# A decoder block in fp32: GLA's output stored ungated and gated in the merge's fetch; shared operands' sums and low parts on VectorE by name, down weights' sums on GpSimd by name

## The chip, the cores and the metric

The kernel runs on one core of one Trainium2 chip, as one program. The metric is the device time of one execution in microseconds. The kernel before has a median of 1993.65 us over 3 runs (1989.53 to 1995.26).

## The reference

One decoder block on 1024 tokens of width 1024, in fp32: a Mamba-2 branch (SSD) and a gated linear attention branch (GLA) side by side, a gated merge, cross attention to 256 memory tokens, and a SwiGLU feed-forward layer (inner width 2816). Cut to what the change touches:

```python
def gla_mixer(q, k, v, r, a1, w_a2, b_a, norm_g):
    ...
    o = (o_intra + o_inter).reshape(Bsz, S, H, dv)
    o = rmsnorm(o, norm_g).reshape(Bsz, S, GLA_DV)
    return (o * jax.nn.silu(r.astype(jnp.float32))).astype(q.dtype)
...
    merged = jax.nn.sigmoid(g_ssd) * (y_ssd @ w_up_ssd) + jax.nn.sigmoid(g_gla) * (y_gla @ w_up_gla)
    return merged @ w_o
...
        h = h + hybrid_mixer(rmsnorm(h, norm_mix[i]), w_in[i], ssd_conv_w[i], ssd_conv_b[i], ssd_dt_bias[i],
                             ssd_A_log[i], ssd_D[i], ssd_norm[i], gla_w_a2[i], gla_b_a[i], gla_norm[i],
                             w_up_ssd[i], w_up_gla[i], w_o[i])
        h = h + mem_cross_attention(rmsnorm(h, norm_xattn[i]), rmsnorm(mem, norm_mem[i]),
                                    w_xq[i], w_xkv[i], w_xo[i])
        h = h + swiglu(rmsnorm(h, norm_ffn[i]), w_ffn_in[i], w_ffn_out[i])
    return rmsnorm(h, norm_final)
```

## The kernel before, in words

**Layout and precision.** Activations are kept transposed: features lie on the 128 partitions, tokens on the free axis (1024, worked in two halves of 512). A matrix of 1024 rows is eight row blocks. A product in fp32 is made of three matmuls: `split` (L223) writes the high part of an operand on ACT (a rounding copy) and its low part on DVE, or on an engine handed to it (a subtraction). Then come high by high, high by low and low by high.

**Two kinds of projections.** `Unit` (L276) with `Operands` (L231) computes a 256-column piece of a projection by seven block products in place of eight, in Winograd's manner. `Operands` holds the right side, shared by all units of a stage: B11, B21, T1, B22, T2, T3, T4, of which the four T's are sums of blocks. `Operands.build` makes for each name and each row block k one sum (`comb`, for the T's) and one split. `Unit.left` makes the sums of weight blocks in the same way (`sa`, `raw`). `dense` (L1191) is the plain form: for each of 16 output tiles 24 matmuls over eight row blocks into one of four PSUM accumulators (`acc`), then `post`.

**Engines by a meter.** `either(ap, slack)` (L85) picks POOL or DVE when the kernel is built, from a rough clock of each engine (`Meter`). It is used in `Operands.build`, `kv_unit`, `v_steps`, `Unit.left`, `presum` and some epilogues. The order of each engine's instructions is then made by the framework's scheduler, from priorities (`ahead`, and `run`, which steps side generators at a rate beside a main one). All DMAs named here are issued by SP, in order, on one queue.

**Stages in time.** 0 to about 190 us: norms of `mem` and `x`, the keys and values of the memory (`kv_unit`, L550, tiles `raw`, `whi`, `wlo`), x turned and scaled into `hs`, the first `Operands` from `hs`, and v with the small columns (`v_steps`, tiles `vraw`, `vsa`). To 640: projections and the SSD scan. 640 to 822: the GLA scan in eight chunks of 128 tokens, beside units of the gates `gs` and `gg`. 837 to 1185: four dense stages (w_up_ssd, w_up_gla, w_o, w_xq). Then cross attention, a fifth dense stage (w_xo), whose output tiles `o` feed the second `Operands`, and the feed-forward layer from about 1330 to the end.

**The GLA scan** (class `GLA`, L998). A chunk loads q and k (`qk`), the decays (`bd`), r (`sr`, 512 KB, written to `sr_d` earlier) and v. `decay` makes exponentials on ACT; `attend` the scores; `out` the output `o`, its mean square, and `o` scaled by its root (ACT, L1067); `norm` turns `o` on PE, and DVE multiplies it with the gain and with Silu(r), which `gate` (L1018) has made on ACT, into `qk`, stored to `yg_d`. ACT loads a function table when it changes between Silu and Exp.

**The merge.** `fetch` (L1213) loads a row block of `ys_d` or `yg_d` into an `hl` tile of 128 x 2 x 1024 and splits it there. The first dense stage computes on `ys_d` while `fetch(yg_d, ...)` runs as a side generator; its epilogue `post_ys` multiplies with Sigmoid of the gate (`gated`, L1286) and stores `ysg_d`. The second adds its own gated product to that and splits it for w_o. The third adds the residual (`residual`, L1300). Gate tiles are `gates` and the weight ring's `whi` and `wlo` (`gate`, L1270); 512-column tiles come from a pool of six, `ga` (`quad`, L1137).

**The down weights.** `presum` (L1239) loads 11 blocks of `in_w_ffn_out` of 1 MB into `pre`, makes four sums of each (`sa`, `pre`) and stores them to `down_d`, beside the first dense stages; `waiting(early, 5)` starts it five steps into the first.

Of the kernel before, what the change touches and what calls it, by code (L numbers as in the profile page):

```python
# [9 lines left out]
F32 = mybir.dt.float32  # L10
# [68 lines left out]
def block_kernel(ctx: ExitStack, tc: tile.TileContext, t: dict, out: bass.AP):  # L79
# [151 lines left out]
    class Operands:  # L231
# [30 lines left out]
        def build(s, hb, kh, first):  # L262
            blk = hb if callable(hb) else lambda: hb
            for name in s.order:
                new, of, comb = s.PLAN[name]
                o = s.B[name] = [slot(s.last_key if name == "T4" else s.key, (P, kh, HALF), F32R, name=name + x) for x in "hl"]
                for k in range(kh):
                    q = lambda ij: blk()[ij[0] * kh + k][:, half(ij[1] ^ s.swap)]
                    for ij in new:
                        first(ij[0] * kh + k, ij[1] ^ s.swap, q(ij))  # L270
                    if comb:
                        comb[0](either(q(of), 1.0), q(of), q(comb[1]), q(comb[2]))
                    split(q(of), o[0][:, k], o[1][:, k], either(q(of)))
                    yield
# [275 lines left out]
    def kv_unit(c0):  # L550
# [7 lines left out]
        for kk in range(4):  # L558
            with ahead():
                hi, lo = wring()  # L560
                hv = hi[:, :512].rearrange("p (k c) -> p k c", c=256)
                lv = lo[:, :512].rearrange("p (k c) -> p k c", c=256)
                split(raw[:, 2 * kk:2 * kk + 2, :], hv, lv, either(lo))
# [73 lines left out]
    def v_steps():  # L637
        for pr in range(2):
# [13 lines left out]
            for n, name in enumerate(CHAIN):  # L652
                parts = []
                with ahead():
                    e = either(A11, 2.0)
                    if name == "T1":
                        add(e, sa, A21, A22)
                    elif name == "B22":
                        sub(e, sa, sa, A11)
                        sub(either(A11, 2.0), A12, A12, sa)  # L660
                    elif name == "T3":
                        sub(e, A21, A11, A21)
# [335 lines left out]
    class GLA:  # L998
# [5 lines left out]
        def load_qk(s):  # L1004
            s.qk = gl.tile([P, 8, CH], F32, name="qk", tag="qk", bufs=2)
# [3 lines left out]
        def load(s):  # L1009
# [3 lines left out]
            s.sr = gl.tile([P, 8, CH], F32, name="sr", tag="sr", bufs=2)  # L1013
            SP.dma_start(s.sr, sr_d[:, tk].rearrange("(k p) s -> p k s", p=P))
            s.v = gl.tile([P, D], F32, name="v", tag="v", bufs=2)
            SP.dma_start(s.v, v_d[tk, :])

        def gate(s):  # L1018
            ACT.activation(s.sr, s.sr, AF.Silu)
# [49 lines left out]
        def norm(s):  # L1069
            for a in range(2):  # L1070
                p = bank()
                for b in range(4):
# [3 lines left out]
                y, g = (x.rearrange("p (b a) s -> p a b s", a=2)[:, a] for x in (s.qk, s.sr))  # L1076
                DVE.scalar_tensor_tensor(y, p.rearrange("p (b s) -> p b s", s=CH), col("gla_norm", a), g,
                                         ALU.mult, ALU.mult)
            SP.dma_start(yg_d[:, s.tk].rearrange("(k p) s -> p k s", p=P), s.qk)

    def gla_steps():
# [10 lines left out]
        it[0].gate()  # L1092
        yield
        for i, a in enumerate(it):
# [4 lines left out]
            if b and i:  # L1099
                b.load_qk()  # L1100
# [10 lines left out]
            if b:  # L1111
                b.gate()
# [113 lines left out]

    get_ys = fetch(ys_d, i_ys, "ssd_norm")
# [11 lines left out]
    def presum():  # L1239
# [3 lines left out]
        for k in range(KP):  # L1243
# [5 lines left out]
            e = lambda: either(s1_, 1.0)  # L1249
            add(e(), s1_, a(1, 0), a(1, 1))  # L1250
            put(0, s1_)
            yield
            sub(e(), a(1, 1), s1_, a(0, 0))
            put(1, a(1, 1))
            yield
            sub(e(), a(1, 0), a(0, 0), a(1, 0))
            put(2, a(1, 0))
            yield
            sub(e(), a(0, 1), a(0, 1), a(1, 1))
# [26 lines left out]
    def gated(g, p):  # L1286
        ACT.activation(g, g, AF.Sigmoid)
        mul(DVE, g, p, g)
# [11 lines left out]
    def residual(store, stats, gain, put):  # L1300
        def post(o, j, p, q):
            add(DVE, q, p, q)
# [18 lines left out]
    run(dense(0, i_ys, post_ys, lambda o, j: gate(gs_d, o, j)), (fetch(yg_d, i_yg), 0.5), (waiting(early, 5), 1.0))  # L1321
    run(dense(1, i_yg, post_yg, lambda o, j: (gate(gg_d, o, j), quad(ysg_d, o * P, 0, j))), (early, 1.0))
    run(dense(2, i_wo, residual(h1_d, s1, "norm_xattn", put_xq), quad_of(xT_d)), (early, 1.0))


# [356 lines left out]
```

## Time and profile before

| | |
|---|---|
| median of 3 runs | 1993.65 us (1989.53 to 1995.26) |
| the profiled execution | 1992.12 us |
| its span in the trace | 1990.4 us |
| granted TensorE clock, mean | 0.992 |
| PE busy | 1933.6 us |
| DVE, ACT, POOL busy | 1315.8, 867.6, 659.7 us |
| read from and written to HBM | 211.07 and 96.80 MB |

The profiled execution is one run, with its own time; the span runs from its first to its last instruction. In the profile's rows an instruction is named by engine, line, operation, and tiles as out<-in. L73 and L51 are lines of the helper classes through which DVE's, POOL's and PE's instructions pass, so there the tiles tell the place. A row of the timeline has its start, its length, and behind it how long the engine was idle before, with what ended that. "x3" means three instructions shown as one row.

### The profile page before, as it was taken

What the parts mean: (1) busy time and instruction counts of PE and PEld (TensorE: products, weight loads), DVE (VectorE), ACT (ScalarE), POOL (GpSimd) and SP (SyncE); (2) the same over time, 40 slices, a digit from 0 to 9 for tenths busy, and PEclk for the clock granted to TensorE, in tenths of its full rate; (3) what the DMA queues carried; (4) which work ended last, traced back from release to release, by engine and by line L of the source; (5) the groups of instructions that cost most, each with busy time, mean ns of one, the idle gap of its engine ahead of it and who ended that gap; (6) DMA issues with size and microseconds to landing.
All of it is one profiled execution on the core that took longest, in us unless ns stands there. A gap on an engine that the chain in (4) does not pass through costs nothing.

```text
span 1990.4 us, 26272 instructions
## 1 busy us (share of the span) xinstructions
PE 1933.6 (97%) x9772; PEld 1619.8 (81%) x9772; DVE 1315.8 (66%) x1837; ACT 867.6 (44%) x1486; POOL 659.7 (33%) x482
## 2 busy tenths in 40 slices
PE   7899999999999999999999999999999999999998
PEld 6899677787887887888888888877888888878887
DVE  6856579978887665643654227478777777784565
ACT  7434845455552555442223226453333333353243
POOL 3521243445654211122442100255444444420002
PEclk9899999999999999999999999999999999999999
DMA  9332233365563756697774210433224224176463
GB/s 311 137 118 88 95 118 117 106 212 169 179 183 101 217 175 185 214 377 254 253 269 158 70 43 22 153 121 102 80 90 148 80 86 130 60 276 215 155 227 126
DMA packets 242019, 309.59 MB, mean 156 GB/s; under 512 B 16586, under 2 KB 164276, under 8 KB 241892
## 3 DMA queue, kind: packets, MB, share of 16 engines
q1 hardware_dynamic: 241892, 307.92, 46.2%
q8 instruction: 77, 1.26, 0.3%
q14 instruction: 50, 0.41, 0.1%
HBM read 211.07 MB, written 96.80 MB: 155 GB/s over the span
## 4 chain that ended last, share of the span: by engine, by line
PE 71%; DVE 11%; ACT 5%; DMA 5%; issue 4%; POOL 3%; SPq 1%; POOLq 0%; DVEq 0%; ACTq 0%
PE acc L51 63%; PE bank L51 8%; DVE wlo L73 2%; DVE cv L73 2%; DMA raw<-in_w_in_dram 1%; DVE o L73 1%; PE bank L55 1%; ACT whi L224 1%; DMA xt<-in_x_dram 1%; DMA sr<-sr_d 1%; DVE fs L73 1%; DMA fr<-act_d 1%; POOL raw L73 1%; POOL sa L73 1%; DMA yg_d<-qk 1%
## 5 line engine op out<-in xcount | busy, mean ns | idle before, releaser
L51 PE MATMUL acc<-hl,wd 128*128 128x512 f32 x1920 | 438.6, 389 | 0.0
L51 PEld LDWEIGHTS acc<-hl,wd 128*128 128x128 f32 x1920 | 360.1, 188 | 74.3
L73 DVE TENSOR_TENSOR wlo<-raw,whi 128x512 fp32r<-128x512 f32 x264 | 242.3, 922 | 75.5 <-ACT whi L224 75.2
L224 ACT ACTIVATE whi<-raw 128x512 fp32r<-128x512 f32 x272 | 169.6, 627 | 233.9 <-PE acc L51 203.1
L73 DVE TENSOR_TENSOR o<-acc,o 128x512 f32<-128x512 f32 (+1 forms) x256 | 172.8, 676 | 113.7 <-PE acc L51 99.5
L51 PE MATMUL acc<-fs 128*128 128x512 f32 (+1 forms) x792 | 156.0, 356 | 1.7 <-ACT o L1577 1.6
L73 POOL TENSOR_TENSOR raw<-raw,sa 128x512 f32<-128x512 f32 x48 | 65.2, 1358 | 260.9 <-DVE wlo L73 252.3
L51 PEld LDWEIGHTS acc<-fs 128*128 128x128 f32 x792 | 130.7, 189 | 22.8 <-ACT o L1577 2.0
L224 ACT ACTIVATE fs<-fr 128x1024 fp32r<-128x1024 f32 (+1 forms) x84 | 79.9, 984 | 112.8 <-PE acc L51 39.8
L73 DVE TENSOR_TENSOR fs<-fr,fs 128x1024 fp32r<-128x1024 f32 (+1 forms) x84 | 99.7, 1219 | 39.2 <-ACT fs L224 38.9
L224 ACT ACTIVATE whi<-sa 128x512 fp32r<-128x512 f32 x96 | 59.9, 626 | 108.0 <-PE acc L51 106.9
L73 POOL TENSOR_TENSOR sa<-raw 128x512 f32<-128x512 f32 x47 | 77.4, 1647 | 78.4 <-DMA raw<-in_w_in_dram 41.1
L73 DVE TENSOR_TENSOR wlo<-sa,whi 128x512 fp32r<-128x512 f32 x96 | 83.6, 873 | 17.7 <-ACT whi L224 16.2
L224 ACT ACTIVATE wd<-raw 128x1024 fp32r<-128x1024 f32 x40 | 42.4, 1059 | 108.7 <-PE acc L51 105.6
L73 DVE TENSOR_TENSOR wd<-raw,wd 128x1024 fp32r<-128x1024 f32 x40 | 54.9, 1373 | 50.5 <-ACT wd L224 50.2
L73 POOL TENSOR_TENSOR raw<-raw 128x512 f32<-128x512 f32 x48 | 83.4, 1738 | 4.7 <-DVE sa L73 4.7
L51 PE MATMUL acc<-B21h,whi 128*128 128x512 f32 x192 | 76.1, 396 | 3.2 <-ACT o L353 3.2
L51 PE MATMUL acc<-T4h,whi 128*128 128x512 f32 x192 | 76.7, 399 | 1.5 <-DVE o L73 1.5
L51 PE MATMUL acc<-B11h,whi 128*128 128x512 f32 x192 | 75.6, 394 | 2.3 <-ACT whi L224 2.3
L51 PE MATMUL acc<-B22h,wlo 128*128 128x512 f32 x192 | 76.2, 397 | 1.2 <-DVE wlo L73 1.2
L51 PE MATMUL acc<-T1h,whi 128*128 128x512 f32 x192 | 75.6, 394 | 1.7 <-ACT whi L224 1.7
L73 POOL TENSOR_TENSOR o<-o 128x512 f32<-128x512 f32 x29 | 49.2, 1702 | 83.4 <-DVE o L73 72.1
(389 smaller groups left out, 4784.6 us busy)
## 6 DMA issues: line engine op xcount, KB each, us to landing
raw<-in_w_in_dram SPq DMA_DIRECT2D x26, 1024.0 KB, 6.0
raw<-in_w_ffn_in_dram SPq DMA_DIRECT2D x22, 1024.0 KB, 6.1
act_d<-o SPq DMA_DIRECT2D x77, 256.0 KB, 2.1
fr<-act_d SPq DMA_DIRECT2D x35, 512.0 KB, 6.6
pre<-in_w_ffn_out_dram SPq DMA_DIRECT2D x11, 1024.0 KB, 7.4
fr<-down_d SPq DMA_DIRECT2D x20, 512.0 KB, 3.7
down_d<-pre SPq DMA_DIRECT2D x33, 256.0 KB, 4.5
raw<-in_w_xkv_dram SPq DMA_DIRECT2D x8, 1024.0 KB
```

Of the source, the lines that this page charges most:

```text
L51: return s.e.matmul(o, x, y, **kw)
L55: return s.e.transpose(o, x, i)
L73: return f(*a, **kw)
L224: ACT.activation(hi, src, AF.Copy)
```

## The change

Four edits.

1. **Shared operands.** In `Operands.build` the sums and low parts, in `kv_unit` the low parts, and in `v_steps` the sums run on DVE always, where the meter chose before. In the order of instructions this moves from POOL to DVE: 14 sums of `hs`, 8 low parts of the memory's weights, four sums of 128x1056 in `v_steps`, the first operands' low parts that POOL had, and eight operations on `o` at the second `Operands`.
2. **GLA.** The scan no longer loads `sr` nor computes Silu; `norm` evicts the turned `o` by a copy on ACT (16 in all) in place of DVE's multiplication, and `yg_d` holds the ungated output. `qk` has three buffers, loaded one chunk earlier. `fetch_gated` takes the place of `fetch(yg_d, ...)`: for each half row block it loads r, makes Silu (ACT), multiplies with output and gain (DVE) and splits. It makes 16 steps, at a rate of 1.0 for 8 at 0.5, and its r tiles come from the pool `ga`.
3. **The gates.** Sigmoid(x) becomes tanh(x/2) on ACT and (t + 1) * p on DVE, which is twice the gated product; the residual after w_o is scaled by 0.5.
4. **Down weights.** The sums of `presum` run on POOL by name; it starts 12 steps into the first dense stage, and its rate in the next two is 1.1.

The number of matmuls is the same. ACT has 18 table loads for 33.

```diff
--- before.py
+++ after.py
@@ -269,8 +269,8 @@
                     for ij in new:
                         first(ij[0] * kh + k, ij[1] ^ s.swap, q(ij))
                     if comb:
-                        comb[0](either(q(of), 1.0), q(of), q(comb[1]), q(comb[2]))
-                    split(q(of), o[0][:, k], o[1][:, k], either(q(of)))
+                        comb[0](DVE, q(of), q(comb[1]), q(comb[2]))
+                    split(q(of), o[0][:, k], o[1][:, k])
                     yield
 
     class Unit:
@@ -560,7 +560,7 @@
                 hi, lo = wring()
                 hv = hi[:, :512].rearrange("p (k c) -> p k c", c=256)
                 lv = lo[:, :512].rearrange("p (k c) -> p k c", c=256)
-                split(raw[:, 2 * kk:2 * kk + 2, :], hv, lv, either(lo))
+                split(raw[:, 2 * kk:2 * kk + 2, :], hv, lv)
             for i in range(2):
                 o = pa[i][:, :256]
                 for k2 in range(2):
@@ -652,14 +652,13 @@
             for n, name in enumerate(CHAIN):
                 parts = []
                 with ahead():
-                    e = either(A11, 2.0)
                     if name == "T1":
-                        add(e, sa, A21, A22)
+                        add(DVE, sa, A21, A22)
                     elif name == "B22":
-                        sub(e, sa, sa, A11)
-                        sub(either(A11, 2.0), A12, A12, sa)
+                        sub(DVE, sa, sa, A11)
+                        sub(DVE, A12, A12, sa)
                     elif name == "T3":
-                        sub(e, A21, A11, A21)
+                        sub(DVE, A21, A11, A21)
                     a = (A11, A12, sa, A12, sa, A21, A22)[n]
                     for k2 in range(2):
                         hi, lo = wring()
@@ -1002,7 +1001,7 @@
             s.c, s.tk = c, slice(c * CH, (c + 1) * CH)
 
         def load_qk(s):
-            s.qk = gl.tile([P, 8, CH], F32, name="qk", tag="qk", bufs=2)
+            s.qk = gl.tile([P, 8, CH], F32, name="qk", tag="qk", bufs=3)
             for i, d in enumerate((q_d, k_d)):
                 SP.dma_start(s.qk[:, 4 * i:4 * i + 4], d[:, s.tk].rearrange("(k p) s -> p k s", p=P))
 
@@ -1010,13 +1009,8 @@
             tk = s.tk
             s.bd = gl.tile([P, 4, CH], F32, name="bd", tag="bd", bufs=2)
             SP.dma_start(s.bd, bd_d[:, tk].rearrange("(k p) s -> p k s", p=P))
-            s.sr = gl.tile([P, 8, CH], F32, name="sr", tag="sr", bufs=2)
-            SP.dma_start(s.sr, sr_d[:, tk].rearrange("(k p) s -> p k s", p=P))
             s.v = gl.tile([P, D], F32, name="v", tag="v", bufs=2)
             SP.dma_start(s.v, v_d[tk, :])
-
-        def gate(s):
-            ACT.activation(s.sr, s.sr, AF.Silu)
 
         def decay(s):
             e = gl.tile([P, 4, CH], F32, name="e", tag="e", bufs=1)
@@ -1073,9 +1067,8 @@
                     k = 2 * b + a
                     PE.transpose(p[:, b * P:(b + 1) * P], s.o[:, k // 2, (k % 2) * P:(k % 2) * P + P], ident)
 
-                y, g = (x.rearrange("p (b a) s -> p a b s", a=2)[:, a] for x in (s.qk, s.sr))
-                DVE.scalar_tensor_tensor(y, p.rearrange("p (b s) -> p b s", s=CH), col("gla_norm", a), g,
-                                         ALU.mult, ALU.mult)
+                ACT.activation(s.qk.rearrange("p (b a) s -> p a b s", a=2)[:, a], p.rearrange("p (b s) -> p b s", s=CH),
+                               AF.Copy)
             SP.dma_start(yg_d[:, s.tk].rearrange("(k p) s -> p k s", p=P), s.qk)
 
     def gla_steps():
@@ -1089,15 +1082,14 @@
         it[0].start()
         yield
         it[0].attend()
-        it[0].gate()
         yield
         for i, a in enumerate(it):
             b = it[i + 1] if i + 1 < len(it) else None
             c = it[i + 2] if i + 2 < len(it) else None
             a.out()
             yield
-            if b and i:
-                b.load_qk()
+            if c:
+                c.load_qk()
             a.scan()
             yield
             if b:
@@ -1108,8 +1100,6 @@
             yield
             if b:
                 b.attend()
-            if b:
-                b.gate()
             if c:
                 c.load()
             yield
@@ -1224,6 +1214,19 @@
                 sub(DVE, x[:, 1], raw, x[:, 0])
             yield
 
+    def fetch_gated(src, gate_src, dst):
+
+        for k in range(NB):
+            x = hl(dst, k)
+            raw = x[:, 1].bitcast(F32)
+            SP.dma_start(raw, src[k * P:(k + 1) * P, :])
+            for j in range(2):
+                g = quad(gate_src, k * P, 0, j)
+                ACT.activation(g, g, AF.Silu)
+                DVE.scalar_tensor_tensor(g, raw[:, half(j)], col("gla_norm", k % 2), g, ALU.mult, ALU.mult)
+                split(g, x[:, 0, half(j)], x[:, 1, half(j)])
+                yield
+
     get_ys = fetch(ys_d, i_ys, "ssd_norm")
     for n, _ in enumerate(group(gg[3:], B)):
         if n == 0:
@@ -1246,17 +1249,16 @@
             a = lambda i, j: r[:, j, half(i)]
             s1_ = sums["m"].tile([P, HALF], F32, name="sa", tag="sa", bufs=2)
             put = lambda n, ap: SP.dma_start(down_d[(n * KP + k) * P:(n * KP + k + 1) * P, :], ap)
-            e = lambda: either(s1_, 1.0)
-            add(e(), s1_, a(1, 0), a(1, 1))
+            add(POOL, s1_, a(1, 0), a(1, 1))
             put(0, s1_)
             yield
-            sub(e(), a(1, 1), s1_, a(0, 0))
+            sub(POOL, a(1, 1), s1_, a(0, 0))
             put(1, a(1, 1))
             yield
-            sub(e(), a(1, 0), a(0, 0), a(1, 0))
+            sub(POOL, a(1, 0), a(0, 0), a(1, 0))
             put(2, a(1, 0))
             yield
-            sub(e(), a(0, 1), a(0, 1), a(1, 1))
+            sub(POOL, a(0, 1), a(0, 1), a(1, 1))
             put(3, a(0, 1))
             yield
 
@@ -1284,8 +1286,8 @@
         return got_g[n][j]
 
     def gated(g, p):
-        ACT.activation(g, g, AF.Sigmoid)
-        mul(DVE, g, p, g)
+        ACT.activation(g, g, AF.Tanh, scale=0.5)
+        DVE.scalar_tensor_tensor(g, g, 1.0, p, ALU.add, ALU.mult)
 
     def post_ys(o, j, p, g):
         gated(g, p)
@@ -1297,9 +1299,9 @@
         add(either(g), g, g, y)
         into(i_wo, o, j, g)
 
-    def residual(store, stats, gain, put):
+    def residual(store, stats, gain, put, scale=1.0):
         def post(o, j, p, q):
-            add(DVE, q, p, q)
+            DVE.scalar_tensor_tensor(q, p, scale, q, ALU.mult, ALU.add)
             SP.dma_start(store[o * P:(o + 1) * P, half(j)], q)
             put(o, j, q, col(gain, o))
             stats.take(j, q)
@@ -1318,9 +1320,9 @@
             yield
 
     early = presum()
-    run(dense(0, i_ys, post_ys, lambda o, j: gate(gs_d, o, j)), (fetch(yg_d, i_yg), 0.5), (waiting(early, 5), 1.0))
-    run(dense(1, i_yg, post_yg, lambda o, j: (gate(gg_d, o, j), quad(ysg_d, o * P, 0, j))), (early, 1.0))
-    run(dense(2, i_wo, residual(h1_d, s1, "norm_xattn", put_xq), quad_of(xT_d)), (early, 1.0))
+    run(dense(0, i_ys, post_ys, lambda o, j: gate(gs_d, o, j)), (fetch_gated(yg_d, sr_d, i_yg), 1.0), (waiting(early, 12), 1.0))
+    run(dense(1, i_yg, post_yg, lambda o, j: (gate(gg_d, o, j), quad(ysg_d, o * P, 0, j))), (early, 1.1))
+    run(dense(2, i_wo, residual(h1_d, s1, "norm_xattn", put_xq, 0.5), quad_of(xT_d)), (early, 1.1))
 
 
     kv = []
```

## The prediction

> **What bounds the kernel now.** First the share of the span for each engine, and the chain of work that ended last, shared out by engine:
>
> ```profile
> span 1990.4 us, 26272 instructions
> PE 1933.6 (97%) x9772; PEld 1619.8 (81%) x9772; DVE 1315.8 (66%) x1837; ACT 867.6 (44%) x1486; POOL 659.7 (33%) x482
> PE 71%; DVE 11%; ACT 5%; DMA 5%; issue 4%; POOL 3%; SPq 1%; POOLq 0%; DVEq 0%; ACTq 0%
> ```
>
> TensorE is busy 97%. The change touches no matmul, so it can only win or lose inside the 1990.4 − 1933.6 = 56.8 us in which PE is idle, or by the clock that a stall costs. So the second view is what PE waits for (us in all, times, longest), and the third the stages that the change touches (stretch, then length and the busy us of PE, PEld, DVE, ACT and POOL, granted clock, DMA share, GB/s).
>
> ```profile
> PE bank L51 <- DVE wlo L73: 6.4, 1, 6.4
> PE bank L55 <- ACT o L1067: 5.6, 4, 2.4
> ...
> 20.00:50.00 30.00, 24.99 (x189) 22.87 (x188) 22.09 (x33) 23.81 (x48) 18.24 (x14) 0.94 0.93 300
> 20.00:70.00 50.00, 36.01 (x256) 33.48 (x256) 42.09 (x48) 32.79 (x66) 36.71 (x25) 0.86 0.82 275
> 41.07:71.51 30.44, 20.58 (x134) 19.47 (x135) 30.44 (x29) 17.70 (x36) 24.07 (x17) 0.78 0.80 287
> 640.00:825.00 185.00, 179.28 (x864) 150.09 (x863) 114.36 (x221) 96.93 (x198) 43.30 (x36) 0.99 0.56 171
> 837.00:925.00 88.00, 88.00 (x390) 72.84 (x390) 38.38 (x38) 35.91 (x46) 18.21 (x12) 1.00 0.90 332
> 840.00:890.00 50.00, 50.00 (x222) 41.42 (x221) 23.95 (x23) 22.42 (x29) 6.07 (x4) 1.00 1.05 397
> 1330.00:1360.00 30.00, 25.92 (x116) 20.61 (x115) 28.78 (x35) 14.85 (x27) 20.41 (x14) 0.94 0.30 97
> ```
>
> Idle PE time: 50 − 36.01 = 13.99 us early, 185 − 179.28 = 5.7 in the GLA scan, none in the first dense stage (837 to 925), 30 − 25.92 = 4.08 at the FFN's start. Early and at the FFN's start DVE is nearly always busy; in the GLA stage PE waits for ACT; in the first dense stage nothing binds but the DMAs run full (397 GB/s).
>
> **Part 1, shared operands by DVE alone, early.** The longest wait, 6.4 us, is here. DVE, POOL, and the chain's pieces of that stretch:
>
> ```profile
> 23.86 0.49 DVE L73 TENSOR_SCALAR diag<-ident,xr 128x128 f32<-128x128 f32 x2 [1.13 <-POOL xr L73]
> 37.20 2.63 DVE L73 TENSOR_SCALAR diag<-ident,xr 128x128 f32<-128x128 f32 x2
> ...
> 43.05 0.68 DVE L73 TENSOR_TENSOR wlo<-raw,whi 128x512 fp32r<-128x512 f32 x1
> 43.65 0.74 DVE L73 SCALAR_TENSOR_TENSOR hs<-bank,cols,rbc 128x512 f32<-128x512 f32 x1
> ...
> 57.39 3.86 DVE L73 TENSOR_TENSOR T1l<-hs,T1h 128x512 fp32r<-128x512 f32 x3
> 72.33 1.89 DVE L73 TENSOR_TENSOR B22l<-hs,B22h 128x512 fp32r<-128x512 f32 x3
> 36.68 2.87 POOL L73 TENSOR_TENSOR vsa<-vraw 128x1056 f32<-128x1056 f32 x1 [2.89 <-DMA vraw<-in_w_in_dram]
> L73 POOL TENSOR_TENSOR hs<-hs 128x512 f32<-128x512 f32 x14 | 22.7, 1652 | 4.5 <-DVE B11l L73 3.3 <-DVE T1l L73 1.3
> 62.98 6.72 PE bank L51 x34
> 77.00 5.76 PE bank L51 x48
> ```
>
> POOL makes 14 sums of hs, 22.7 us, the bulk of its 24.07 us in 41.07 to 71.51, where DVE never rests. The same DVE operation takes 3.86 us for three while POOL works and 1.89 for three when it doesn't. Alone, a tensor-tensor starts (43.65 − 43.05) 0.60 us before the next. DVE's 29 instructions there are 20 tensor-tensors, 8 scalar-tensor-tensors from PSUM and a small copy: undisturbed 20 × 0.60 + 8 × 0.66 (0.74 less the overlap of 0.08) + 0.2 = 17.5 us. It took 30.44, so 12.9 us of DVE's time go to running beside POOL, 0.92 for each of the 14 sums. Done on DVE a sum costs 0.60: 14 × (0.92 − 0.60) = 4.5 us less on the engine that PE waits for. I take −4.2, since some of POOL's time there (24.07 − 22.7) stays.
> The stall also costs clock: after it, 34 matmuls take 6.72 us (0.198 each) against 5.76 for 48 (0.12), 34 × 0.078 = 2.7 us. A wait shorter by two thirds should save about half: −1.3.
> The kv lows and two sums of 128x1056 go to DVE too. The latter takes 2.87 us on POOL; on DVE I scale 0.60 by 1056/512 to about 1.25 and see the disturbance come back: diag 2.63 beside it against 0.49. I take these moves as even. Sum early: −5.5. Bounds: −12, if nearly all of the 13.99 idle goes (the rest are first loads), and +3, if DVE's extra work comes ahead of what PE needs next, as the first kv low after the stall stands ahead of T1's lows in the new order.
> A rule bears on this. The Trainium skill, "SBUF — State Buffer", section "Who interferes with whom", says that a DVE instruction with two SBUF inputs and a GpSimd instruction that reads SBUF exclude one another, the loser waiting for the whole instruction. By it each sum could cost DVE nearly all of its time on POOL; the 0.92 that the trace gives lies below that. It makes the gain larger (first rival).
>
> **Part 2, the GLA scan.** Groups of ACT and DVE in 640 to 825 (busy, mean ns; then idle before them and its releaser):
>
> ```profile
> L1019 ACT ACT_TABLE_LOAD x8 | 10.3, 1283 | 25.7 <-DMA sr<-sr_d 25.6
> L1019 ACT ACTIVATE sr<-sr 128x1024 f32<-128x1024 f32 x8 | 8.5, 1060 | 0.1
> L1034 ACT ACTIVATE kt<-bank 128x512 f32<-128x512 f32 x8 | 4.8, 596 | 6.9 <-PE bank L55 6.9
> L73 DVE SCALAR_TENSOR_TENSOR qk<-bank,cols,sr 128x512 f32<-128x512 f32 x16 | 11.2, 742 | 1.9 <-PE bank L55 1.9
> ```
>
> Per chunk ACT loses a Silu (1.06), the two table loads around it (2 × 1.28) and 25.6/8 = 3.2 us of waiting at its head for sr: 6.8 us. It gains two PSUM evictions like kt's (2 × 0.60), which stand behind PE's transposes as DVE's did; DVE loses 16 × 0.74. PE's 5.6 us in this stage all wait for ACT's o, which is queued behind these. I take −5: most of 5.6. Bounds −6.4 (all, with a little clock) and +3 (the 16 copies hold o up by 0.2 us each). qk gets a third buffer and is asked for a step earlier; no PE wait on it is seen, so 0.
>
> **Part 3, gating in the first dense stage.** DMA issues on SP, the fetch of ys on ACT, and PE's first matmuls of the stage:
>
> ```profile
> 820.26 1.43 SPq L1218 DMA_DIRECT2D hl<-ys_d  x2
> 821.77 1.43 SPq L1156 DMA_DIRECT2D raw<-in_w_up_ssd_dram  x2
> 826.38 5.57 SPq L1218 DMA_DIRECT2D hl<-ys_d  x6
> 835.14 7.48 ACT L1220 ACTIVATE hl<-hl,cols 128x1024 fp32r<-128x1024 f32 x6 [0.18 <-DMA hl<-ys_d]
> 837.50 2.88 PE L51 MATMUL acc<-hl,wd 128*128 128x512 f32 x12
> 859.46 0.69 DVE L73 TENSOR_TENSOR gates<-acc,gates 128x512 f32<-128x512 f32 x1 [2.75 <-PE acc L51]
> ```
>
> Six sr loads (0.26 MB), two gate loads (0.5) and one of the down weights (1 MB) now stand on SP ahead of the last ys: 3.67 MB more, at 397 GB/s 9.2 us later. The last high part ended at 835.14 + 7.48 = 842.6; it would end at 851.8. In the new order PE does 84 matmuls (72 on four accumulators, 12 of T4) before it needs ys block 6. The stage does 390 in 88.00, 0.226 us each; 84 are 19.0, from 834.8 (12 before 837.50): needed at 853.8, the last block 2.7 later. It holds with 2 to 5 us to spare. The four accumulators then end together: four evictions of 0.69 against 12 matmuls (2.7): +0.3. ACT's 16 Silus, tanhs and copies and DVE's 16 more multiplications go into their 52 and 50 us of idle time in 837 to 925. Without the cover it costs up to the whole 9.2. Bounds 0 to +9.2.
> Beside it, the Trainium skill's "SBUF — State Buffer", section "Summary: rules for kernel authors", estimates HBM transfers at about 358 GB/s. By that the 3.67 MB would take 10.3 us, and the margin shrinks; the trace's 397 GB/s disagrees.
>
> **Part 4, the FFN's start, and the down weights.**
>
> ```profile
> 1331.03 4.08 DVE L73 TENSOR_TENSOR T2l<-o,T2h 128x512 fp32r<-128x512 f32 x3
> 1330.52 3.44 POOL L73 TENSOR_TENSOR B22l<-o,B22h 128x512 fp32r<-128x512 f32 x2
> 1336.54 4.87 POOL L73 TENSOR_TENSOR o<-o 128x512 f32<-128x512 f32 x3 [2.59 <-ACT o L1472]
> L73 POOL TENSOR_TENSOR pre<-pre 128x512 f32<-128x512 f32 x22 | 36.6, 1682 | 0.0
> L73 POOL TENSOR_TENSOR pre<-sa,pre 128x512 f32<-128x512 f32 x11 | 14.9, 1356 | 0.9
> L73 POOL TENSOR_TENSOR sa<-pre 128x512 f32<-128x512 f32 x11 | 14.2, 1288 | 148.7 <-DMA pre<-in_w_ffn_out_dram 63.9 <-DMA hl<-yg_d 59.6 <-DMA gates<-gg_d 16.0
> ```
>
> In 1330 to 1342 five operations, 8.31 us of POOL, become 5 × 0.60 = 3.0 us of DVE, while three T2 lows beside them take 4.08 instead of 1.89. By the early price the five save 5 × (0.92 − 0.60) = 1.6 us, with some clock −2; bounds −4.1 (all the idle time) and +2 (DVE, 28.78 of 30 us busy, gets later).
> The down weights' 22 + 11 + 11 = 44 sums are already all on POOL, so naming it moves only their start. They use 65.7 us there, and in the new order the last stands ahead of the loads for the cross attention: 0.
>
> **The sum.** −5.5 − 5 + 0.3 − 2 = −12.2 us on the profiled execution: 1990.4 of span plus 1.7 around it, 1992.1, becomes 1979.9. The median of the runs lies 1.5 above it, 1993.65, so I forecast 1981. About 0.3%, 6 us, is what can be told from no change: faster is below 1987.7, slower above 1999.6.
>
> **The rivals.**
> 1. More is gained, 1971: all touched idle time goes, 12 + 6.4 + 4.1 = 22.5. For it: DVE gets its full time back if each sum costs it the 1.29 us of the undisturbed `sa<-pre`, 14 × (1.29 − 0.60) = 9.7. Against: T1 to T4 still wait for DVE's own work. By the Trainium skill's rule above this is what should happen.
> 2. The stalls only move, 1990: early, PE waits for the kv low and then for T1l, and ACT's copies hold o as Silu did; only a third of the sum, 4, is left. For it: the kv low stands ahead in DVE's order.
> 3. The last ys land late, 1990.6: the 9.2 us show at PE in full, 1981.4 + 9.2. For it: the DMA share is 1.05 there. Against: the 84 matmuls.
> 4. DVE alone becomes the bound, 2002: its long durations are its own, not POOL's, so each moved operation adds its whole time. The operations moved early (14 sums, 8 kv lows, four of about 1.25) are 22 × 0.60 + 5.0 = 18.2 us; DVE's idle time in 20 to 50 takes 30 − 22.09 = 7.9 of it: +10.3. At the FFN's start +3, the GLA scan −5: +8.3. It decides from the point where POOL's sums cost DVE less than 0.60 each. Against: 3.86 and 1.89.
> 5. The change doesn't do what it says for the down weights: true already, and priced 0.
>
> **How the numbers follow.** Forecast 0.53, rival 1 0.12, 2 0.13, 3 0.07, 4 0.15. The forecast's own range is 1976 to 1987; 8 in 10 need both neighbours, and the bounds of the early stage reach to rival 4, so 1970 to 2002. Faster: 0.53 + 0.12, less 0.02 for the forecast's tail, 0.63. Slower: rival 4 and a tail, 0.17. Within: 0.20.
>
> **What would show it.** Early: T1l at about 0.65 us each, the wait of PE for the low at 62.98 shrunk from 6.4 to about 2, PE's idle time in 20 to 70 near 9. GLA: no table loads around a Silu, PE's wait for o below 1. First dense stage: PE busy throughout, with the last ys part ending near 852. FFN's start: PE idle near 2 in 30 us. I am wrong if DVE's tensor-tensors stay at 1.2 us or more early without POOL, if PE has a gap before 860 in the first dense stage, or if ACT's copies are what PE waits for in the scan.

## The result, and the profile after

The changed kernel has a median of 1980.35 us over 4 runs (1979.68 to 1982.29). The kernel before has 1992.38 beside it, over 4 runs (1989.53 to 1995.26). The ratio is 0.9941, with a 95% interval of 0.9924 to 0.9958: 11.8 us less (8.4 to 15.1). The forecast was 1981, from −12.2 us. The sum was right; two of its terms were not, and that their errors cancelled is luck.

First the page of the changed kernel: share of the span by engine, and the chain that ended last.

```profile
span 1980.6 us, 26287 instructions
PE 1932.2 (98%) x9772; PEld 1617.0 (82%) x9772; DVE 1323.7 (67%) x1884; ACT 859.5 (43%) x1503; POOL 600.5 (30%) x443
PE 75%; DVE 10%; issue 4%; ACT 4%; DMA 3%; POOL 3%; SPq 1%; POOLq 0%; ACTq 0%; DVEq 0%
```

POOL has 59 us less to do and DVE only 8 more, though DVE does 47 operations more, so others of its operations must have got shorter. PE's idle time falls from 56.8 to 48.4 us. What PE waits for, and the stages (columns as before):

```profile
PE bank L55 <- ACT xs L608: 5.3, 5, 3.8
PE bank L51 <- DVE wlo L73: 3.6, 3, 1.9
...
20.00:70.00 50.00, 41.08 (x293) 37.28 (x293) 40.69 (x71) 35.81 (x73) 3.74 (x4) 0.93 0.87 292
640.00:825.00 185.00, 184.70 (x902) 156.28 (x901) 108.06 (x211) 88.11 (x201) 39.79 (x34) 1.00 0.55 175
840.00:850.00 10.00, 9.39 (x38) 6.44 (x36) 5.91 (x8) 4.86 (x7) 2.51 (x2) 1.00 1.06 393
850.00:860.00 10.00, 9.60 (x43) 7.93 (x43) 8.38 (x13) 4.17 (x8) 0.00 (x0) 1.00 1.04 406
```

The wait of 6.4 us for one low part is 1.5 in its old place (now at 58.3), and the longest such wait is 1.9, at 72.8. A new one stands earlier: 3.8 us, up to 41.7, for ACT's copies of the turned x. They stand on ACT behind a high part that itself waited 3.3 us for a load of the memory's weights. PE's idle time in 20 to 70 is 8.92 us, from 13.99. In the GLA scan it is 0.3, from 5.7. The first dense stage, which had no gap, has two.

DVE in the early stage, in the timeline of the changed kernel:

```profile
40.20 0.47 DVE L73 TENSOR_SCALAR diag<-ident,xr 128x128 f32<-128x128 f32 x2
...
54.94 1.89 DVE L73 TENSOR_TENSOR B21l<-hs,B21h 128x512 fp32r<-128x512 f32 x3
...
58.77 1.29 DVE L73 TENSOR_TENSOR T1l<-hs,T1h 128x512 fp32r<-128x512 f32 x2
...
62.99 1.89 DVE L73 TENSOR_TENSOR hs<-hs 128x512 f32<-128x512 f32 x3
```

Three low parts take 1.89 us where three of the same shape took 3.86, and the sums of hs are here now, three in 1.89 too.

One profile of each kernel is a small sample, and the early stage varies by some 3 us. So the table takes the stage lengths from the profiles of the two kernels and of experiments 1 to 7 and 9, by the first instruction of each stage: those whose order in the stage is the old one against those with the new one. In the changed kernel these are (timelines of PE and DVE; the first of the units that follow the shared operands, here called z, of the SSD's outputs, of the dense stages, of the cross attention):

```profile
168.49 0.40 PE L51 MATMUL acc<-B11h,whi 128*128 128x512 f32 x1
...
417.57 1.11 DVE L73 SCALAR_TENSOR_TENSOR y<-xz,dcol,bank 128x128 f32<-128x128 f32 x4
...
822.12 2.88 PE L51 MATMUL acc<-hl,wd 128*128 128x512 f32 x12
...
1177.03 5.91 PE L51 MATMUL acc<-kvhl,hl 128*128 128x256 f32 x48
```

In the new order 12 matmuls of T4 (2.7 us) come after the first dense matmuls instead of before them; they are taken off the old scan and added to the old dense stages, so that equal work is compared. The kernel of experiment 5 is left out of the two rows of scan and dense stages: it leaves work out of the one, and had two gaps of 2.7 us together near 1088 in the other. The kernel of experiment 4 is left out of the first row and that of experiment 7 out of the third, where they differ on purpose. Experiments 8 and 10 to 12 move more work to DVE everywhere and are in no row.

| stage | old order, us (profiles) | new order, us (profiles) | difference |
|---|---|---|---|
| start to the first z unit | 174.0 (4: 172.2 to 175.8) | 169.1 (5: 168.5 to 169.7) | −4.9 |
| first SSD output to the first dense stage | 414.0 (3: 412.6 to 415.3) | 404.0 (6: 403.1 to 404.6) | −10.0 |
| four dense stages | 352.8 (3: 352.7 to 352.9) | 354.9 (5: all 354.9) | +2.1 |
| feed-forward, to the down weights | 426.72 (5: 426.59 to 426.80) | 425.96 (5: 425.54 to 427.16) | −0.8 |

The differences add up to −13.6 us, where the runs give −11.8 (−8.4 to −15.1). The second row begins in the SSD scan; from the first matmul on q and k to the first dense one, with the 12 matmuls taken off, it is 173.3 us in the kernel before (661.49 to 837.50) and 164.3 in the changed one (657.79 to 822.12).

### The profile page after: what moved, and what is told of

The parts are those of the page before. It is cut to its first block, busy times and chain, and to the rows that moved or that the text cites. A ratio compares the mean times of both kernels' runs of the same rounds, so it can differ in the third digit from the quotient of the medians.

```text
span 1980.6 us, 26287 instructions
## 1 busy us (share of the span) xinstructions
PE 1932.2 (98%) x9772; PEld 1617.0 (82%) x9772; DVE 1323.7 (67%) x1884; ACT 859.5 (43%) x1503; POOL 600.5 (30%) x443
## 4 chain that ended last, share of the span: by engine, by line
PE 75%; DVE 10%; issue 4%; ACT 4%; DMA 3%; POOL 3%; SPq 1%; POOLq 0%; ACTq 0%; DVEq 0%
PE acc L51 65%; PE bank L51 9%; DVE wlo L73 2%; DVE cv L73 2%; DVE o L73 1%; PE bank L55 1%; DMA raw<-in_w_in_dram 1%; DMA xt<-in_x_dram 1%; POOL raw L73 1%; POOL sa L73 1%; DMA fr<-act_d 1%; DVE fs L73 1%; POOL o L73 1%; ACT whi L224 1%; POOL y L73 0%
## 5 line engine op out<-in xcount | busy, mean ns | idle before, releaser
L73 DVE TENSOR_TENSOR wlo<-raw,whi 128x512 fp32r<-128x512 f32 x272 | 248.3, 917 | 77.8 <-ACT whi L224 77.5
L224 ACT ACTIVATE whi<-raw 128x512 fp32r<-128x512 f32 x272 | 169.7, 628 | 245.2 <-PE acc L51 206.5
L73 POOL TENSOR_TENSOR raw<-raw,sa 128x512 f32<-128x512 f32 x48 | 69.2, 1441 | 253.0 <-DVE wlo L73 242.1
L51 PE MATMUL acc<-B22h,whi 128*128 128x512 f32 x192 | 76.2, 397 | 1.1 <-DVE o L73 1.1
```

What stands on the lines that cost most here:

```text
L51: return s.e.matmul(o, x, y, **kw)
L73: return f(*a, **kw)
L224: ACT.activation(hi, src, AF.Copy)
```

## The experiments

Ratios are to the kernel before, run on the same chip; 0.001 is 2 us.

**1. The shared operands alone.**

```diff
-                        comb[0](either(q(of), 1.0), q(of), q(comb[1]), q(comb[2]))
-                    split(q(of), o[0][:, k], o[1][:, k], either(q(of)))
+                        comb[0](DVE, q(of), q(comb[1]), q(comb[2]))
+                    split(q(of), o[0][:, k], o[1][:, k])
...
-                split(raw[:, 2 * kk:2 * kk + 2, :], hv, lv, either(lo))
+                split(raw[:, 2 * kk:2 * kk + 2, :], hv, lv)
...
+                        add(DVE, sa, A21, A22)
```

> The kernel before with the first edit alone (shared operands' sums and low parts, the memory's low parts and v's sums on DVE). Theory (by stage): the early stage gives 4 to 5 us, the FFN's start nothing, so about 1988 against 1992.5 for before, with PE's wait of 6.4 us for one low part gone and its idle time in 20 to 70 near 9 us instead of 14. Rival (the whole change's gain is GLA's, and the early stage only moves its stall): within 2 us of before.

By the traces this takes off POOL 14 sums of hs, 8 low parts of the memory's weights, six sums of 128x1056 (not four), and 7 low parts and 8 sums on o (not eight operations in all); the meter gives POOL four additions of an epilogue in return. No low part of the first operands was on POOL.

Measured: 1991.28 us, ratio 0.9986 (0.9975 to 0.9996), 2.8 us less. That lies between the theory and the rival. The profile has the early stage at 169.45, as in the changed kernel, PE idle for 7.7 us in 20 to 70, and no long wait for a low part:

```profile
PE bank L51 <- DVE wlo L73: 4.0, 4, 2.1
PE bank L55 <- ACT xs L608: 4.0, 4, 3.3
```

The feed-forward stage is 1.2 us shorter, but the last stage of this profile, whose instructions nothing changed, is 2.9 us longer than the 234.6 of most others; so are two other profiles here (experiments 6 and 9), by 2.3 and 2.5. The traces show where: PE waits there once for ACT's copies of its accumulators, 3.1, 2.5 and 2.6 us in these three and 1.6 to 2.1 in the others with this order, and after the longer waits matmuls start 0.43 us apart for a while in place of 0.227 (granted clock 0.66 in 1789 to 1794 here, 1.00 in 1790 to 1795 of the kernel before). Here ACT stood behind a load of the down weights. Why that is late in some executions, and whether this run's other executions had it, is open.

**2. GLA's ungated store and the gating fetch alone.** The edits to `GLA`, `gla_steps` and `fetch_gated`, on the kernel before, with its Sigmoid and its start of the down weights.

> The kernel before with GLA's ungated store, the earlier qk and the gating in the merge's fetch alone (Sigmoid, the meter and the down weights as before). Theory: PE's idle time in the GLA scan goes from 5.7 to under 1 us, the first dense stage gives back about 2 us between its first four output tiles and the next, so 4 to 6 us less than before, about 1987. Rival (the first dense stage's loads come too late without the other edits, since the down weights start earlier here): the stage loses 5 us or more and the sum is even with before.

Measured: 1985.36 us, ratio 0.9956 (0.9941 to 0.9970), 8.8 us less: more than the theory gave. PE doesn't wait for ACT's o at all in 640 to 825, and the first dense stage has the same two gaps (0.60 and 0.40 us). The rival falls.

**3. Tanh and the down weights alone.** The edits to `gated`, `residual`, `presum` and its rates, on the kernel before.

> The kernel before with tanh for Sigmoid and the down weights' edit alone. Theory: PE never waits in the dense stages of the kernel before, so nothing: within 1.5 us of before, with 18 fewer or as many table loads none of which PE waits for. Rival (the later start of the down weights frees HBM in the first dense stage, or the fewer table loads shorten ACT's work): 2 to 3 us less than before.

Measured: 1993.83 us, ratio 0.9994 (0.9984 to 1.0004): nothing that can be told from zero, as the theory has it. The three parts add up to −12.8 us, against −11.8 for the whole.

**4. Sums on POOL that nobody reads.** Does POOL's work cost DVE time, or was the way through POOL and back too long?

```diff
+                        if s.idle is not None:
+                            z = q((0, 1) if name == "T1" else (1, 1))
+                            nc.gpsimd.tensor_tensor(s.idle, z, z, ALU.subtract)
                         comb[0](DVE, q(of), q(comb[1]), q(comb[2]))
```

> The changed kernel with 16 more sums of 128x512 on POOL, one beside each sum of the first shared operands, reading the same hs and writing a tile that nobody reads; the orders of DVE and ACT stay as they are. Theory (POOL's sums cost DVE its own time, about 0.9 us each): DVE's tensor-tensors between 50 and 72 us go from 0.60 to about 1.2 us or more each and the run gets 7 to 14 us longer than the changed kernel, since nothing is taken off DVE in return. Rival (what cost time before was the way through POOL and back, not its running beside DVE): the same time as the changed kernel, within 1.5 us, and DVE's durations unchanged.

Measured: 1992.37 us, ratio 0.9988 (0.9978 to 0.9997): 9.4 us longer than the changed kernel, most of its gain, for 16 operations without a reader. The early stage is 178.9 us long, 9.8 more. The theory holds and the rival falls. POOL and DVE in the timeline of this kernel:

```profile
44.44 6.50 POOL L275 TENSOR_TENSOR idle<-hs 128x512 f32<-128x512 f32 x5 [2.65 <-DVE hs L73]
...
60.06 13.08 POOL L275 TENSOR_TENSOR idle<-hs 128x512 f32<-128x512 f32 x9 [3.16 <-DVE hs L73]
...
47.07 0.74 DVE L73 SCALAR_TENSOR_TENSOR hs<-bank,cols,rbc 128x512 f32<-128x512 f32 x1
...
64.94 1.52 DVE L73 TENSOR_TENSOR hs<-hs 128x512 f32<-128x512 f32 x1
66.38 1.52 DVE L73 TENSOR_TENSOR T1l<-hs,T1h 128x512 fp32r<-128x512 f32 x1
67.83 1.52 DVE L73 TENSOR_TENSOR wlo<-raw,whi 128x512 fp32r<-128x512 f32 x1
...
77.84 0.70 DVE L73 TENSOR_TENSOR wlo<-vraw,whi 128x528 fp32r<-128x528 f32 x1
```

The two engines go in step: a sum of POOL's every 1.45 us (13.08 / 9), a tensor-tensor of DVE's every 1.45 (64.94 to 66.38 to 67.83). It is the operations that take longer, 1.52 us with no idle time between them, a low part of weights too that shares no tile with POOL: so it's not a wait for POOL's result. Alone a tensor-tensor starts 0.60 after the last, so in this stretch each POOL sum costs DVE 0.85 us. The prediction had 0.92, from the profile of before alone. Where DVE never rests, work of its own that costs 0.60 is cheaper than work of POOL's that costs it 0.85.

The Trainium skill, "SBUF — State Buffer", section "Who interferes with whom", says that a VectorE instruction with two SBUF inputs and a GpSimd one that reads SBUF block each other. The step of 1.45 agrees in kind. Beside DVE's operations on PSUM the first of these sums start 1.12 us apart (44.44, 45.56, 46.68); strict turns would take 1.12 + 0.60 = 1.72, so DVE loses somewhat less than a whole sum. (These sums read one tile twice; a sum of two tiles may cost more.)

**5. The scan without its Silu.**

```diff
         def gate(s):
-            ACT.activation(s.sr, s.sr, AF.Silu)
+            pass
```

> The kernel before without the Silu of r in the GLA scan (r itself multiplies the output; its loads stay). Leaves out that function alone. Theory (ACT's Silu, the table loads around it and ACT's wait for sr at its head hold up the output o, for which PE waits): PE's wait for ACT's o in 640 to 825 goes from 5.6 to under 1.5 us, and the run is 5 to 9 us shorter than before. Rival (the gain of the scan lies in r's loads, 4 MB less on the queue and in HBM, or in DVE's multiplication): within 2 us of before.

Measured: 1988.25 us, ratio 0.9968 (0.9956 to 0.9981), 6.4 us less, within what the theory gave. PE's wait in the scan, in this kernel's profile:

```profile
PE bank L55 <- ACT o L1067: 2.1, 1, 2.1
```

It fell from 5.6, but to 2.1, not under 1.5. The profiled execution is the longest of the twelve (1995.53 us), and its dense stages have the two gaps named above, so it shows the scan and not the whole. From the first SSD output to the dense stages it takes 409.4 us, on the measure of the table: about half of the 10 us. The other half goes with the loads of r or with DVE's multiplication, which this kernel keeps; the two were not separated. A pointer to the loads: DVE's waits for q in 640 to 825 are 24.0 us in the kernel before and 27.2 here, and 12.1 in the changed kernel.

**6. Two buffers of qk, loaded late**, in the changed kernel:

```diff
-            s.qk = gl.tile([P, 8, CH], F32, name="qk", tag="qk", bufs=3)
+            s.qk = gl.tile([P, 8, CH], F32, name="qk", tag="qk", bufs=2)
...
-            if c:
-                c.load_qk()
+            if b and i:
+                b.load_qk()
```

> The changed kernel with two buffers of qk, loaded where they were before. Theory (no PE wait hangs on qk): within 1.5 us of the changed kernel, so about 0.994 of before. Rival (the third buffer is a part of the scan's gain, since ACT's copies now write qk late and its store holds the buffer): 3 us or more longer than the changed kernel, 0.9955 of before or above, with PE or DVE waiting for qk.

Measured: 1981.34 us, ratio 0.9930 (0.9915 to 0.9944): no loss. By the ratios it is 2.2 us shorter than the changed kernel, with intervals that overlap. PE's waits in 640 to 825 are 0.3 us, as in the changed kernel, so the third buffer and the earlier load bring nothing that shows. Their counterpart, both in the kernel before, wasn't tried.

**7. r loaded into the output's own tile**, in the changed kernel:

```diff
-            raw = x[:, 1].bitcast(F32)
+            raw, r = x[:, 1].bitcast(F32), x[:, 0].bitcast(F32)
             SP.dma_start(raw, src[k * P:(k + 1) * P, :])
+            SP.dma_start(r, gate_src[k * P:(k + 1) * P, :])
             for j in range(2):
-                g = quad(gate_src, k * P, 0, j)
-                ACT.activation(g, g, AF.Silu)
+                g = rp.tile([P, HALF], F32, name="ga", tag="ga")
+                ACT.activation(g, r[:, half(j)], AF.Silu)
```

> The changed kernel with r loaded, 512 KB at a time, into the high half of the tile that the gated output will fill, in place of 256 KB tiles of the pool ga: its loads can no longer stand ahead of the last ys. Theory (the first dense stage loses about 2 us because 1.5 MB of r come ahead of ys, so that four output tiles end together and DVE's gating comes between their evictions): the two gaps of PE near 846 to 852 shrink and the run is 1 to 2.5 us shorter than the changed kernel, near 0.993 of before. Rival (the loss comes from the gating's work on DVE and ACT, whenever it comes): the same time as the changed kernel or longer.

Measured: 1979.56 us, ratio 0.9925 (0.9909 to 0.9940), 3 us better than the changed kernel by the medians of the ratios, with intervals that overlap. The profile tells more: the windows of this kernel have no gap, and 46 matmuls where the changed kernel has 38 and 43.

```profile
840.00:850.00 10.00, 10.00 (x46) 8.29 (x45) 8.79 (x12) 8.15 (x12) 0.00 (x0) 1.00 1.05 394
850.00:860.00 10.00, 10.00 (x46) 8.29 (x45) 7.54 (x12) 6.57 (x12) 0.00 (x0) 1.00 1.03 408
```

In 837 to 925 it makes 390 matmuls, as many as the kernel before, where the changed kernel makes 381. So the first dense stage's loss came from where r's loads stood: with them later, DVE's gating comes after three of the four evictions. The four dense stages together take 353.6 us, only 1.3 less than in the changed kernel, since two short stalls of PE (near 1075 and 1093) take a part back.

**8. The units' sums of weight blocks on DVE too**, in the changed kernel:

```diff
-            e = either(A11, 2.0)
+            e = DVE
...
-                sub(either(A11, 2.0), A12, A12, s.S2)
+                sub(DVE, A12, A12, s.S2)
```

> The changed kernel with the units' sums of weight blocks on DVE by name as well (186 operations that the meter gives POOL). Theory (a sum on POOL costs DVE about 0.7 us where DVE works, the sum on DVE 0.60, so it's even in DVE's time, and PE seldom waits for DVE in the middle of the kernel): within 3 us of the changed kernel. Rival (the sums on POOL are a net loss everywhere): 5 us or more shorter than the changed kernel, 0.9915 of before or below.

Measured: 1967.21 us, ratio 0.9867 (0.9848 to 0.9886): 14.7 us better than the changed kernel. The theory falls; the rival's time came in, but its reason, that POOL's sums are a net loss, needs a closer look. The low parts of weights in the changed kernel, and then in this one:

```profile
L73 DVE TENSOR_TENSOR wlo<-raw,whi 128x512 fp32r<-128x512 f32 x272 | 248.3, 917 | 77.8 <-ACT whi L224 77.5
```

```profile
L73 DVE TENSOR_TENSOR wlo<-raw,whi 128x512 fp32r<-128x512 f32 x272 | 200.5, 745 | 55.4 <-ACT whi L224 54.9
```

The same 272 operations take 48 us less. DVE's busy time rises from 1323.7 to 1348.1 us, 24 us for 186 more operations, which at 0.60 each would be 112: the other 87 came back from its other work. So among the units a sum on POOL cost DVE 87 / 186 = 0.47 us, less than the theory's 0.7 and less than the 0.60 of doing it itself. In DVE's time the move is a small loss; the theory's error was that PE doesn't feel what POOL lengthens. PE's waits for the weights' high and low parts, in the changed kernel and then in this one:

```profile
PE acc L51 <- ACT whi L224: 5.7, 7, 2.8
PE acc L51 <- DVE wlo L73: 4.1, 13, 0.8
```

```profile
PE acc L51 <- ACT whi L224: 2.9, 5, 1.0
PE acc L51 <- DVE wlo L73: 1.0, 2, 0.8
```

Both fall, and PE's idle time in all goes from 48.4 to 41.6 us. Low parts that POOL's sums lengthened, and that matmuls wait for, are one part of the gain. Another may be that a sum itself is ready sooner on DVE than on POOL (on POOL the 47 sums `sa<-raw` take 1.62 us each), and ACT's high part with it; the two weren't separated.

**9. The second shared operands by the meter again**, in the changed kernel: `either` back in `Operands.build`, for the order that begins B11, T1 alone.

> The changed kernel with the second shared operands (those of the feed-forward layer) by the meter again: eight operations on o go back to POOL. As predicted, the edit gave 2 us at the FFN's start, so without it 2 us longer than the changed kernel, with PE idle about 4 us in the 40 us from the layer's start. Theory after the result (PE's idle time there was 4.1 us before and after): within 1.5 us of the changed kernel.

Measured: 1985.24 us, ratio 0.9950 (0.9936 to 0.9963). By the ratios it is 1.8 us longer than the changed kernel, with intervals that overlap: neither side is settled by time. PE is idle for 4.0 us in the 40 us from the layer's start, as the first side has it, and for 3.0 in the changed kernel. (15 operations on o go back to POOL, as counted in experiment 1.) By the table's stage it takes 426.7 us, like all profiles with this order, and four of five with the new one take 425.5 to 425.8 (the changed kernel's own profile is the exception). So the edit is worth about 1 us. DVE's T2 lows here and in the changed kernel:

```profile
1321.49 4.09 DVE L73 TENSOR_TENSOR T2l<-o,T2h 128x512 fp32r<-128x512 f32 x3
```

```profile
1321.59 1.88 DVE L73 TENSOR_TENSOR T2l<-o,T2h 128x512 fp32r<-128x512 f32 x3
```

DVE is relieved as it was early, but PE's idle time in this stage is bound elsewhere too (its wait for ACT's first copies of the accumulators fell from 2.4 to 1.3 us, and one for DVE of 1.1 came in).

**10. The units' sums on DVE in the kernel before**, with nothing of the change: the edit of experiment 8.

> The kernel before with the units' sums of weight blocks on DVE by name, and nothing of the change. Theory (a two-operand sum on POOL holds up DVE's two-operand instructions wherever they meet, and through them the weights' low parts that PE is about to use): 10 to 18 us shorter than before, as the changed kernel gained by it, with the mean of DVE's low parts of weights down from 0.92 to about 0.75 us. Rival (the gain needs the change's early stage, where POOL is already free): under 5 us.

Measured: 1982.30 us, ratio 0.9935 (0.9920 to 0.9949), 13.0 us less: within what the theory gave, and as much as the whole change gains. The low parts' mean falls from 922 to 758 ns, and DVE's busy time rises by 12.1 us for 184 more operations, so a sum on POOL had cost it 0.53. The gain doesn't need the change's early stage.

**11. The edits of experiments 7 and 8 together.**

> The changed kernel with the units' sums on DVE and r loaded into the gated output's own tile, both together. Theory (separate stages, so they add): 0.9853 of before, 1 to 3 us shorter than with the units' sums alone. Rival (the first dense stage is hidden by something else once the rest is faster): the same as with the units' sums alone, 0.9867.

Measured: 1966.25 us, ratio 0.9861 (0.9844 to 0.9879), 27.7 us better than the kernel before and 16 better than the changed one. Against experiment 8 the difference is within the intervals, and the dense stages are not shorter in its profile (355.8 against 355.4 us): that they add isn't shown.

**12. All that the meter places, on DVE.** On top of experiment 11, `either` returns DVE always.

> The same, with every operation that the meter places on DVE (86 more, most in the epilogues of the feed-forward layer); POOL keeps the down weights' sums, the sums of squares and small work. Theory (in the layer PE is already busy all the time, so DVE's gain or loss is hidden): within 3 us of the kernel without it. Rival 1 (POOL's operations still cost more than they save): 4 us or more shorter. Rival 2 (DVE becomes the bound): 4 us or more longer, with PE waiting for DVE's low parts in 1340 to 1730.

Measured: 1966.60 us, ratio 0.9858 (0.9845 to 0.9871): the same as 11. The time is within the theory's range, but the one profile doesn't show its reason, that the layer hides the move. There the feed-forward stage takes 420.8 us and the last stage 231.9, where the profile of 11 has 422.7 and 234.5: 4.5 us shorter. The four dense stages take 359.8 for 355.8, with a wait of PE of 3.5 us near 1064 for ACT's high part of the weights. The two cancel. Whether that wait belongs to the edit is open: experiment 5's kernel, without this edit, has one of 2.0 us for the same reason at the same place, some 250 us after the first dense matmul.

## Why the prediction was right, step by step

**Early, −5.5 forecast, −4.9 found.** The mechanism is shown by experiment 4, with 0.85 us for the predicted 0.92. The signs named came in: T1's low parts at 0.65 us each, PE's wait for a low part at 1.5 to 1.9, its idle time in 20 to 70 at 8.9. What wasn't foreseen is that the stall would partly move to an earlier place, to ACT's copies of x (3.8 us).

**The GLA scan, −5 forecast, −10.0 found.** This is the term that was mis-sized, "most of 5.6", and the result lies beyond its own bound of −6.4. The chain was right as far as it goes (no table loads around a Silu are left in the scan, PE's wait for o is 0.3 us, and experiment 5 gives about half of the gain by the Silu alone). But the 5.6 us were read from the view of waits as if PE lost no more. Windows of the kernel before, the first of them ahead of the scan:

```profile
645.00:660.00 15.00, 15.00 (x69) 12.45 (x68) 10.35 (x21) 6.81 (x11) 3.00 (x4) 1.00 0.77 225
...
705.00:720.00 15.00, 13.22 (x62) 10.55 (x61) 6.72 (x18) 8.90 (x19) 1.04 (x1) 1.00 0.57 172
720.00:735.00 15.00, 15.00 (x69) 13.01 (x67) 9.19 (x18) 7.53 (x13) 5.07 (x4) 0.89 0.72 213
735.00:750.00 15.00, 15.00 (x79) 12.85 (x78) 8.57 (x18) 6.78 (x18) 1.02 (x1) 1.00 0.56 170
765.00:780.00 15.00, 12.63 (x61) 10.40 (x60) 7.15 (x19) 8.93 (x20) 2.80 (x3) 1.00 0.52 153
```

The bare counts can't be compared, since the windows hold different matmuls: the first has nearly only those 512 columns wide, and is smooth with 69, as many as the one from 720 with its clock of 0.89. So each kind is taken at its own undisturbed step in this trace: 0.227 us for 512 columns, 0.216 for 256 and 0.11 for 128. By these the matmuls that start in the windows from 705, 720, 735 and 765 fill 12.4, 13.3, 15.0 and 12.1 of the 15 us: 2.6, 1.7, 0 and 2.9 us are lost, where the idle time shows 1.78, 0, 0 and 2.37. Over the whole scan, from the first matmul on q and k to the first dense one, 468, 192 and 160 of the three kinds fill 165.3 of 176.0 us: 10.7 are lost. In the changed kernel, with 12 of 512 columns fewer, 1.7 of 164.3 are. The idle time, 5.7, was little more than half of the loss.

**The first dense stage, +0.3 forecast, +2.1 found.** The loads came out as worked out: the last high part of ys was to end 17.0 us after the first dense matmul (851.8 − 834.8), and it did (838.01 + 1.15 less 822.12). PE didn't wait for it. The step that failed is "four evictions of 0.69 against 12 matmuls". With it came a sign that the prediction had named for being wrong, a gap of PE before 860 in this stage. PE and DVE in the changed kernel:

```profile
827.56 19.95 PE L51 MATMUL acc<-hl,wd 128*128 128x512 f32 x86
848.11 1.93 PE L51 MATMUL acc<-hl,wd 128*128 128x512 f32 x6 [0.59 <-DVE gates L73]
850.44 19.79 PE L51 MATMUL acc<-hl,wd 128*128 128x512 f32 x86 [0.40 <-DVE wd L73]
...
845.44 0.69 DVE L73 SCALAR_TENSOR_TENSOR gates<-gates,acc 128x512 f32<-128x512 f32 x1 [4.09 <-PE acc L51]
846.05 1.41 DVE L73 SCALAR_TENSOR_TENSOR ga<-hl,cols,ga 128x512 f32<-128x512 f32 x2
847.37 1.88 DVE L73 SCALAR_TENSOR_TENSOR gates<-gates,acc 128x512 f32<-128x512 f32 x3
849.17 2.35 DVE L73 TENSOR_TENSOR wd<-raw,wd 128x1024 fp32r<-128x1024 f32 x2
```

The four tiles end together, as forecast, but two multiplications of the gating stand between the first eviction and the others, and the low part of the next weight block, which PE needs, stands behind them all. The prediction counted DVE's spare time over the stage (50 us) and not its order at this one place. Here too the matmuls tell more than the gaps: the 92 from 827.56 to 850.44 take 22.88 us, where 92 × 0.226 is 20.8, so 2.1 are lost, and the gaps are 1.0.

**The feed-forward's start, −2 forecast, about −1 found** (experiment 9; PE is idle for 3.0 us in the stage's first 30, and the prediction's sign was 2); **the down weights and tanh, 0 forecast, −1.2 within its interval found** (experiment 3).

So an undersized gain in the scan (5 us) paid for a loss in the dense stage (1.8 us more than forecast), a smaller gain at the feed-forward's start (1 us) and a little of the early one. The direction and the chains of the two large terms were understood; that the sum came within 1 us was luck. The rivals: the stall did move in part, but the early stage still gained; the loads were late by what was worked out and hidden; DVE alone did not become the bound, and experiments 8 and 10 show that it had room for 186 operations more.

## What to carry to other kernels

Where POOL's two-operand sums run beside DVE's two-operand work, POOL's idle time isn't free. Packed together, a sum on POOL took 0.85 us from DVE here, more than the 0.60 of doing it on DVE. Nor does that price decide alone: spread among the units a sum on POOL took only about 0.5 us from DVE, and moving it still gained 13 to 15 us. So ask first whether what POOL lengthens or delays is something that a matmul waits for. Size a stall by the matmuls that a stretch is short of, each kind at its own undisturbed step, and not by the idle time or by the bare count. Work fitted into an engine's spare time needs its place in the order checked where several results fall due at once.

## What was not expected of the hardware

The size of the gain from sums on DVE: 184 operations that POOL does in its idle time cost the kernel before 13.0 us (experiment 10), though PE's idle time there fell by 6.2 us only (56.8 to 50.6). A DVE instruction that reads one operand from PSUM and one from SBUF beside POOL's sums kept its 0.74 us (the row at 47.07 in experiment 4, inside POOL's five sums from 44.44 to 50.94), where those with two operands in SBUF went to a step of 1.45. And the last stage, with an unchanged order, took either about 234.6 or about 237 us in the profiles: in the longer ones a wait of PE was 0.4 to 1.5 us longer, and matmuls ran slower for a while after it, in experiment 1 at a granted clock of 0.66.
